# Differential attention: coefficients once per head, scores one step ahead, five items beside the value slice, and the last rotations inside the loop

## The chip, the core and the metric

The kernel runs on one core of a Trainium2 chip. The metric is the device time of one execution in microseconds (us). In the profile PE is TensorE (matmul), PEld its weight loads, DVE is VectorE, ACT is ScalarE, POOL is GpSimd and SP is SyncE.

## What is computed

The program is one inference step of a four-layer transformer trunk on 384 tokens (128 context tokens and 256 latent tokens), model width 1024. Each layer is a token mixer followed by a SwiGLU network, both modulated by shift, scale and gate vectors from a linear map of a condition (`w_ada`). Only layer 0, differential attention, is touched by the change:

```
q, k, v = split(h @ w_qkv)                    # 1024 columns each
q = rms_norm(q per 64), k = rms_norm(k per 64)
q, k = apply_rope(q), apply_rope(k)           # latent tokens only
s = einsum(q[head, map], k[head, map]) / 8    # 8 heads, 2 maps each
p = softmax(s)
a = p[map 0] - lam * p[map 1]
o = rms_norm(a @ v[head]) * 0.2 * gain
out = o @ w_o
```

Context queries see the 128 context keys, latent queries see 128 cached and 256 latent keys.

## The kernel before, in words

**Projection.** Weights arrive in units of 1024 columns, are cast by ScalarE (`wh`, L234), and VectorE subtracts the cast for the low part (`wl`, L244). Three matmuls per product (high x high, low x high, high x low) restore precision. In layer 0 `proj_slices` computes four slices of 512 columns, in eight steps k each: queries 0 to 511, keys 512 to 1023, queries 512 to 1023, and last the second half of the values, here called the **value slice**. What a slice leaves to do (`post`, `post_norm`: statistics, a scaling L878, the rotations L891 to L910, the transposes L918 and their copies L923) is a list of functions, and the next slice calls one of them in each of its steps. The value slice accumulates in PSUM banks 3, 5 and 7, and after it ScalarE copies these out (`put_v`, L944).

**Attention.** There are 24 **items**: 8 heads, and for each three blocks of 128 queries in the order 1, 2, 0. Blocks 1 and 2 have 384 keys (wide items), block 0 has 128 (narrow items). For an item two score matmuls (L977, one per map) fill two of four banks; VectorE takes two maxima (L991); ScalarE does two exponentials with their sums (L1000); VectorE forms the reciprocal of one sum (L1005), the coefficient (L1009) and the combination of the two maps (L1015); TensorE transposes it (L1032), ScalarE copies that (L1034), TensorE multiplies by the values (L1063). After a head's last item come sums of squares on ScalarE (L1091), a chain of small operations on three numbers (L1105 to L1115), a scaling (L1117), a transpose (L1127) and the split into `oh` (L1128) and `ol` (L1129), the input of the output projection `w_o` (L396 to L398).

**Order.** `at(e, rank, f)` puts a function into **step** e, and `advance()` issues one step, sorted by rank. PE, DVE and ACT run exactly in the order written, in the loop. `IL0` says how many steps are issued in each k of the value slice; the rest run in a loop of their own up to step 24, and what is left is called between the first matmuls of `w_o`.

**Fill.** Products of the `w_ada` map are mixed in by `fill`. Some entries run on TensorE: a product (L337), a copy on ScalarE (L340), a turn (L346), a copy on VectorE (L347). Others are two passes of VectorE over 128x1024 numbers (L328). The small transposes, products and turns share a ring `tr` of two banks, 6 and 7.

Of the kernel before, what the change touches and what calls it, by code (L numbers as in the profile page):

```python
# [42 lines left out]
IL0 = (0,0,0,0,0,0,1,0)  # L43
ADA_PE = ((4, 0), (4, 1), (4, 3), (4, 4), (4, 5), (4, 7), (3, 0), (3, 1), (3, 3), (3, 4), (3, 5), (3, 7))
ADA_QKV = ((0, 0, 1, 0, 0, 0, 1, 0),) * 4
ADA_A = (((0.5,1),),((0.5,1),),((1.6,2),),(),((0.5,1),),((1.6,2),))
# [13 lines left out]
RK = (1.0, 1.1, 1.2, 1.3, 1.5, 2.5, 5.5)  # L60
DBANKS = dict(acc=(4, 5, 1, 2, 3), tr=(7, 0, 6))
RMS_AT = 1
ATT_A = (2, 3, 1, 1, 2, 1, 0)
# [86 lines left out]
def trunk(ctx: ExitStack, tc: tile.TileContext, a):  # L150
# [161 lines left out]
    def ada_parts():  # L312
# [31 lines left out]
        def turn(row):  # L344
            t = tbank()
            T.matmul(out=t[:, 0:2], lhsT=row, rhs=quarter, start=True, stop=True)  # L346
            V.tensor_copy(out=out, in_=t[:, 0:2])  # L347
# [6 lines left out]
        if pe:  # L354
            row = []
            return [lambda: row.append(product()), lambda: (turn(row[0]), finish())]
# [406 lines left out]
    def attn_layer(li, att, nd):  # L763
# [184 lines left out]
        def post(i, ps):  # L948
            if diff:
                if i == 3:  # L950
                    return [put_v(ps, 0, 512, 512), lambda: None]
                return post_norm(ps, i % 2, 512, 8, i // 2 * 4 + i % 2 * 4)
# [4 lines left out]
        events, state, out, last = {}, {}, {}, [None]  # L957

# [5 lines left out]
        def stats_of(c):  # L964
            if ("st", c) not in state:
                state["st", c] = sm.tile([128, 8, 6], F32, name="ast", tag="ast", bufs=3)
# [26 lines left out]
        def exps(i, c, t):  # L993
            st_ = stats_of(c)
            state["p", i] = []
            for m, ps in enumerate(state.pop(("s", i))):
                j = 2 * t + m
                w = ps.shape[1]
                p = att.tile([128, TOK + 1], F32, name="p", tag="p")
# [3 lines left out]
        def inverse(i, c, t):  # L1003
            j = slice(2 * t + int(diff), 2 * t + 2)
            V.reciprocal(out=stats_of(c)[:, 2, j], in_=stats_of(c)[:, 1, j])  # L1005

        def coefficient(i, c, t):
            st_ = stats_of(c)
            V.scalar_tensor_tensor(out=st_[:, 2, 2 * t:2 * t + 1], in0=st_[:, 1, 2 * t:2 * t + 1], scalar=neglam,  # L1009
                                   in1=st_[:, 2, 2 * t + 1:2 * t + 2], op0=ALU.mult, op1=ALU.mult)  # L1010
# [124 lines left out]
        def fill(what):  # L1135
# [3 lines left out]
            elif what and ad["done"] < min(len(adas), ad["limit"]):  # L1139
                pe = adas[ad["done"]][3]  # L1140
                f, f2 = ada_parts()
                f()
                (half_done if pe else halves).append(f2)

        def fill_end():
            while half_done:
                half_done.pop()()
# [559 lines left out]
```

## Time and profile before

| | |
|---|---|
| median of three runs | 1896.53 us (1895.76 to 1897.22) |
| profiled execution, its own time | 1896.06 us |
| its span, first to last instruction | 1894.3 us |
| PE busy in the span | 1867.7 us (99%) |
| DVE / ACT busy in the span | 1518.5 us / 901.6 us |
| first score matmul / last one | 125.4 us / 185.6 us |

The span leaves out 1.8 us around the first and the last instruction. Times inside a profile count from the start of the span.

### The profile page before, as it was taken

How to read it: one execution, taken by the hardware profiler on the slowest of the kernel's cores; microseconds unless marked ns; L12 is line 12 of the kernel's file. 1: busy time of each engine (PE TensorE's matmuls, PEld its weight loads, DVE VectorE, ACT ScalarE, POOL GpSimd, SP SyncE). 2: the span in 40 equal slices, each digit the busy share in tenths (PEclk: the TensorE clock that was granted, in tenths of full speed). 3: DMA queues.
4: the chain of work that ended last, by engine and by line, in shares of the span. 5: the costliest groups of instructions: out<-in, count | busy, mean ns of one | idle time of the engine just before them, and what ended most of it. 6: DMA issues, size and time to landing. Idle time of an engine off the chain costs nothing.

```text
span 1894.3 us, 29902 instructions
## 1 busy us (share of the span) xinstructions
PE 1867.7 (99%) x11200; PEld 1744.2 (92%) x11200; DVE 1518.5 (80%) x2980; ACT 901.6 (48%) x1764; POOL 109.3 (6%) x207
## 2 busy tenths in 40 slices
PE   9998999999999999999999999999999999999999
PEld 6876999999975999999975999999989989999999
DVE  6999899995688999994688999994758897964442
ACT  6458553233558553234468553233556665632331
POOL 0011001110000001110000001110000000000000
PEclk9999999999999999999999999999999999999999
DMA  9664568775330568774330558774433324554442
GB/s 374 221 190 141 156 191 261 259 258 165 112 117 1 173 187 263 256 256 144 109 117 1 178 187 269 248 240 128 122 112 119 108 87 140 170 167 129 120 126 67
DMA packets 90742, 315.93 MB, mean 167 GB/s; under 512 B 10977, under 2 KB 14945, under 8 KB 90341
## 3 DMA queue, kind: packets, MB, share of 16 engines
q1 hardware_dynamic: 63508, 217.86, 35.7%
q0 software_dynamic: 26656, 95.97, 16.3%
q8 instruction: 88, 1.44, 0.3%
q14 instruction: 58, 0.47, 0.1%
q10 hardware_dynamic: 432, 0.20, 0.0%
HBM read 309.78 MB, written 4.20 MB: 166 GB/s over the span
## 4 chain that ended last, share of the span: by engine, by line
PE 87%; DVE 6%; ACT 4%; issue 2%; DMA 1%; POOL 0%; ACTq 0%; DVEq 0%; SPq 0%; POOLq 0%
PE b L396 24%; PE b L398 24%; PE b L397 24%; PE b L629 2%; PE b L630 2%; PE b L633 2%; PE b L515 2%; ACT p L1000 1%; PE b L977 1%; PE b L1079 1%; DMA ada<-in_ada_dram 1%; PE b L1051 1%; DVE ast L991 1%; PE b L918 1%; DVE junk L328 1%
## 5 line engine op out<-in xcount | busy, mean ns | idle before, releaser
L244 DVE TENSOR_TENSOR wl<-raw,wh 128x1024 fp32r<-128x1024 f32 x384 | 467.3, 1222 | 155.3 <-ACT wh L234 154.9
L234 ACT CAST wh<-raw 128x1024 fp32r<-128x1024 f32 x384 | 399.2, 1047 | 352.4 <-PE b L397 201.2
L398 PE MATMUL b<-fhh,wl 128*128 128x384 f32 x1280 | 433.9, 339 | 0.0
L397 PE MATMUL b<-fhl,wh 128*128 128x384 f32 x1280 | 432.4, 338 | 0.0
L396 PE MATMUL b<-fhh,wh 128*128 128x384 f32 x1280 | 432.4, 338 | 0.0
L328 DVE CUSTOM_DVE_ANT_0 junk<-ada,condb 128x1024 bf16<-128x1024 f32 x312 | 380.3, 1219 | 2.6 <-DMA ada<-in_ada_dram 0.2
L398 PEld LDWEIGHTS b<-fhh,wl 128*128 128x128 f32 x1280 | 241.8, 189 | 0.0
L397 PEld LDWEIGHTS b<-fhl,wh 128*128 128x128 f32 x1280 | 241.8, 189 | 0.0
L396 PEld LDWEIGHTS b<-fhh,wh 128*128 128x128 f32 x1280 | 241.5, 189 | 0.0
L396 PE MATMUL b<-fh,wh 128*128 128x384 f32 x704 | 239.0, 339 | 0.0
L398 PE MATMUL b<-fh,wl 128*128 128x384 f32 x704 | 237.4, 337 | 0.0
L397 PE MATMUL b<-fl,wh 128*128 128x384 f32 x704 | 237.4, 337 | 0.0
L700 ACT CAST fh<-w 128x384 fp32r<-128x384 f32 x88 | 45.2, 514 | 288.8 <-DVE w L706 280.8
L396 PE MATMUL b<-xh,wh 128*128 128x386 f32 (+1 forms) x448 | 155.1, 346 | 0.0
L398 PE MATMUL b<-xh,wl 128*128 128x386 f32 (+1 forms) x448 | 152.6, 341 | 0.0
L397 PE MATMUL b<-xl,wh 128*128 128x386 f32 (+1 forms) x448 | 151.5, 338 | 0.0
L299 POOL DMA_DIRECT2D ada<-in_ada_dram x176 | 93.4, 531 | 985.5 <-DVE mod L328 840.4
L398 PEld LDWEIGHTS b<-fh,wl 128*128 128x128 f32 x704 | 132.3, 188 | 0.0
L397 PEld LDWEIGHTS b<-fl,wh 128*128 128x128 f32 x704 | 132.2, 188 | 0.0
L396 PEld LDWEIGHTS b<-fh,wh 128*128 128x128 f32 x704 | 132.2, 188 | 0.0
L413 DVE SCALAR_TENSOR_TENSOR x<-b,mod,x 128x128 f32<-128x128 f32 x192 | 69.6, 411 | 40.3 <-PE b L398 40.3
L706 DVE TENSOR_TENSOR w<-b,w 128x384 f32<-128x384 f32 x80 | 44.4, 555 | 58.4 <-PE b L398 58.2
(267 smaller groups left out, 2850.5 us busy)
## 6 DMA issues: line engine op xcount, KB each, us to landing
raw<-in_w_dram SPq DMA_DIRECT2D x384, 512.0 KB, 4.2
ada<-in_ada_dram POOLq DMA_DIRECT2D x176, 512.0 KB, 4.7
a0s<-in_ada_dram SPq DMA_DIRECT2D x8, 512.0 KB, 9.8
ada<-in_ada_dram SPq DMA_DIRECT2D x8, 512.0 KB, 9.9
x<-in_x_dram SPq DMA_DIRECT2D x4, 384.0 KB, 4.7
out_y_dram<-x SPq DMA_DIRECT2D x8, 192.0 KB, 1.9
condb<-saved SPq DMA_DIRECT2D x1, 1024.0 KB, 11.4
s<-in_state_dram POOLq DMA_DIRECT2D x8, 128.0 KB, 2.3
```

Of the source, the lines that this page charges most:

```text
L234: S.copy(out=hi, in_=st["raw"][u])
L244: V.tensor_tensor(out=lo, in0=st["raw"].pop(u), in1=st["hi"][u].bitcast(F32), op=ALU.subtract)
L299: (nc.gpsimd if i >= 16 else nc.sync).dma_start(out=t, in_=a["ada"][i])
L328: V.tensor_tensor_reduce(out=ad["junk"], in0=raw, in1=ad["cond"][:, j, :], op0=ALU.mult, op1=ALU.add, scale=1.0, scalar=0.0, accum_out=out ...
L396: T.matmul(out=out, lhsT=lh, rhs=rh, start=start, stop=False)
L397: T.matmul(out=out, lhsT=lh, rhs=rl, start=False, stop=False)
L398: T.matmul(out=out, lhsT=ll, rhs=rh, start=False, stop=stop)
L413: V.scalar_tensor_tensor(out=x[:, d, c0:c1], in0=ps[:, c0:c1], scalar=gate[:, d, j:j + 1], in1=x[:, d, c0:c1], op0=ALU.mult, op1=ALU.add)
L515: T.matmul(out=ps[3 * i + t], lhsT=xs[:, k, t * 128:t * 128 + 128], rhs=ws, start=p == 0 and k == 0, stop=p == 2 and k == KC - 1)
L629: T.matmul(out=ps[t], lhsT=hh[:, k, c], rhs=wh, start=k == 0, stop=False)
L700: S.copy(out=fh[:, j, :], in_=m)
L706: V.tensor_tensor(out=m, in0=up[:, :TOK], in1=sg, op=ALU.mult)
```

## The change

- The reciprocals and coefficients of a head's three items are formed by one operation each (`coefficients`), two steps after the head's last item was issued.
- Scores are issued one step ahead: maxima and exponentials of item i move from step i to step i+1, the combination from i+1 to i+4, the transpose from i+2 to i+5, the product with the values from i+3 to i+6.
- Steps 0 to 4 are issued in k = 3 to 7 of the value slice (before: step 0 in k = 6).
- The rotations and transposes of the last query slice leave the value slice and are called one per step after steps 5 to 10.
- `fill` is called once per step from step 5 on, and the turn of a TensorE entry and its copy are placed one step later, at ranks 0.4 and 1.6.
- The second map's exponentials go to the ring `w`, and the statistics have five buffers in another pool.

```diff
-IL0 = (0,0,0,0,0,0,1,0)
+IL0 = (0,0,0,1,1,1,1,1)
-ADA_A = (((0.5,1),),((0.5,1),),((1.6,2),),(),((0.5,1),),((1.6,2),))
+ADA_FROM = 5
-RK = (1.0, 1.1, 1.2, 1.3, 1.5, 2.5, 5.5)
+RK = (1.0, 1.1, 1.2, 1.3, 1.5, 0.4, 1.6)
-ATT_A = (2, 3, 1, 1, 2, 1, 0)
+ATT_A = (5, 6, 4, 1, 1, 1, 0)
...
-            return [lambda: row.append(product()), lambda: (turn(row[0]), finish())]
+            return [lambda: row.append(product()), lambda: row.append(turn(row[0])), lambda: (keep(row[1]), finish())]
...
+                fs = post_norm(ps, i % 2, 512, 8, i // 2 * 4 + i % 2 * 4)
+                if i == 2:
+                    turns.extend(fs[3:4] + fs[6:7] + fs[4:5] + fs[7:8] + fs[2:3] + fs[5:6])
+                    return fs[:2]
+                return fs
...
-                p = att.tile([128, TOK + 1], F32, name="p", tag="p")
+                p = work(TOK) if diff and m else att.tile([128, TOK + 1], F32, name="p", tag="p", bufs=6 if diff else 7)
...
-        def coefficient(i, c, t):
+        def coefficients(c):
             st_ = stats_of(c)
-            V.scalar_tensor_tensor(out=st_[:, 2, 2 * t:2 * t + 1], in0=st_[:, 1, 2 * t:2 * t + 1], scalar=neglam,
-                                   in1=st_[:, 2, 2 * t + 1:2 * t + 2], op0=ALU.mult, op1=ALU.mult)
+            V.reciprocal(out=st_[:, 2, 1:6:2], in_=st_[:, 1, 1:6:2])
+            V.scalar_tensor_tensor(out=st_[:, 2, 0:6:2], in0=st_[:, 1, 0:6:2], scalar=neglam,
+                                   in1=st_[:, 2, 1:6:2], op0=ALU.mult, op1=ALU.mult)
...
-                at(i + 1, RK[0], inverse, *args)
-                at(i, RK[1], maxima, 0, *args)
-                at(i + 1, RK[2], coefficient, *args)
-                at(i, RK[3], maxima, 1, *args)
-                at(i + 1, RK[4], combine, *args)
-                at(i, 3, exps, *args)
-                for rank, what in ADA_A[i % len(ADA_A)]:
-                    at(i, rank, fill, what)
-                at(i + int(RK[6] < 0), abs(RK[6]), fill_end)
+                at(i + 1, RK[1], maxima, 0, *args)
+                if i % 3 == 2:
+                    at(i + 2, 1.0, coefficients, c)
+                at(i + 1, RK[3], maxima, 1, *args)
+                at(i + cl, RK[4], combine, *args)
+                at(i + 1, 3, exps, *args)
+                if i >= ADA_FROM:
+                    at(i, 2.6, fill, 2)
+                at(i + 1, RK[5], fill_end, 0)
+                at(i + 1, RK[6], fill_end, 1)
...
-            pend = proj_slices(li, hh, hl, list(enumerate(slice_cols(li))), post, ids, step, pend)
+            pend = proj_slices(li, hh, hl, list(enumerate(slice_cols(li))), post, ids, step, pend) + turns
```

Lines below L347 have other numbers in the changed file: L977 is L986 there, L991 L1000, L1000 L1009, L1015 L1026, L1032 L1043, L1063 L1074, L944 L947, L629 to L633 are L632 to L636, L347 L350 and L1129 L1140. The new reciprocal is L1019, the new coefficient L1020.

ScalarE where the value slice ends and the loop begins, before: the last transposed queries (`qT`), the three copies of the values, a row of a fill product, the two exponentials of item 1 and those of item 2.

```order
L923 COPY qT<-b_1312 128x4x128
L944 COPY vt<-b_1138 128x512
L944 COPY vt<-b_1139 128x512
L944 COPY vt<-b_1140 128x512
L340 COPY row<-b_1339 128x128
L1000 ACTIVATE p,ast<-b_1335,ast 128x384
L1000 ACTIVATE p,ast<-b_1336,ast 128x384
L1000 ACTIVATE p,ast<-b_1364,ast 128x128
L1000 ACTIVATE p,ast<-b_1365,ast 128x128
```

The same place after the change: the exponentials of item 3, the copies of the values, a row, those of item 4, the first transposed item, a second row and those of item 5.

```order
L1009 ACTIVATE p,ast<-b_1272,ast 128x384
L1009 ACTIVATE w,ast<-b_1273,ast 128x384
L947 COPY vt<-b_1138 128x512
L947 COPY vt<-b_1139 128x512
L947 COPY vt<-b_1140 128x512
L340 COPY row<-b_1335 128x128
L1009 ACTIVATE p,ast<-b_1297,ast 128x384
L1009 ACTIVATE w,ast<-b_1298,ast 128x384
L1045 COPY pt<-b_1352 128x384
L340 COPY row<-b_1373 128x128
L1009 ACTIVATE p,ast<-b_1328,ast 128x128
L1009 ACTIVATE w,ast<-b_1329,ast 128x128
```

The exponentials of items 0 to 3 now stand ahead of the copies of the values, and those of item 4 behind them and behind the row of a product.

VectorE in the middle of the loop before, two steps of one head: small operations stand between the two maxima of an item.

```order
L347 COPY mod<-b_1770 128x2
L1005 RECIPROCAL ast<-ast 128x1
L991 TENSOR_REDUCE ast<-b_1773 128x1
L1009 SCALAR_TENSOR_TENSOR ast<-ast,lam 128x1
L991 TENSOR_REDUCE ast<-b_1774 128x1
L1015 SCALAR_TENSOR_TENSOR p<-p,ast 128x384
L328 ISA junk,mod<-ada,condb 128x1024
L328 ISA mod 128x1
L1129 SCALAR_TENSOR_TENSOR ol<-b_1793,subg,oh 128x384
L1005 RECIPROCAL ast<-ast 128x1
L991 TENSOR_REDUCE ast<-b_1804 128x1
L1009 SCALAR_TENSOR_TENSOR ast<-ast,lam 128x1
```

VectorE at the corresponding two steps after the change.

```order
L350 COPY mod<-b_1742 128x2
L1000 TENSOR_REDUCE ast<-b_1738 128x1
L1000 TENSOR_REDUCE ast<-b_1739 128x1
L1026 SCALAR_TENSOR_TENSOR p<-w,ast,p 128x384
L350 COPY mod<-b_1783 128x2
L328 ISA junk,mod<-ada,condb 128x1024
L328 ISA mod 128x1
L1140 SCALAR_TENSOR_TENSOR ol<-b_1800,subg,oh 128x384
L1000 TENSOR_REDUCE ast<-b_1779 128x1
L1000 TENSOR_REDUCE ast<-b_1780 128x1
```

The reciprocal and the coefficient are gone from these steps; one pair of them stands at the head of every third step.

TensorE in the value slice after the change, from the start of k = 4 (bank numbers 1138 to 1140 are the value slice's accumulators, 1209 and 1210 the scores of item 0, 1222 and 1223 those of item 1).

```order
L986 MATMUL b_1223<-kT,qT 128x384
L632 MATMUL b_1138<-wh,hh 128x512
L633 MATMUL b_1138<-wl,hh 128x512
L632 MATMUL b_1139<-wh,hh 128x512
L633 MATMUL b_1139<-wl,hh 128x512
L986 MATMUL b_1209<-kT,qT 128x384
L986 MATMUL b_1210<-kT,qT 128x384
L632 MATMUL b_1140<-wh,hh 128x512
L986 MATMUL b_1222<-kT,qT 128x384
```

Before, no scores stood here; the first ones stood between k = 5 and k = 6.

## Rows read from the trace of the kernel before

**Rows 1.** Windows by stage: each engine's busy us, PE clock, DMA share.

```profile
104.00:125.00 21.00, 21.00 (x100) 17.16 (x99) 21.00 (x36) 7.57 (x13) 1.61 (x3) 1.00 0.68 214
125.00:132.30 7.30, 7.30 (x52) 4.93 (x50) 5.58 (x12) 4.52 (x10) 1.06 (x2) 1.00 0.49 150
132.30:186.00 53.70, 46.16 (x452) 32.03 (x452) 48.84 (x178) 42.80 (x176) 7.95 (x15) 1.00 0.48 150
186.00:200.00 14.00, 14.00 (x92) 13.85 (x92) 11.14 (x33) 6.73 (x27) 1.59 (x3) 1.00 0.54 175
```

**Rows 2.** DVE groups by line and shape, 132 to 186 us: busy, mean ns, idle before.

```profile
L991 DVE TENSOR_REDUCE ast<-b 128x1 f32<-128x384 f32 x30 | 16.4, 547 | 1.4 <-PE b L977 1.3
L1015 DVE SCALAR_TENSOR_TENSOR p<-p,ast 128x384 f32<-128x384 f32 x15 | 9.1, 609 | 0.0
L328 DVE CUSTOM_DVE_ANT_0 junk<-ada,condb 128x1024 bf16<-128x1024 f32 x7 | 8.5, 1219 | 0.2 <-DMA ada<-in_ada_dram 0.2
...
L991 DVE TENSOR_REDUCE ast<-b 128x1 f32<-128x128 f32 x14 | 3.9, 277 | 0.0
L1005 DVE RECIPROCAL ast<-ast 128x1 f32<-128x1 f32 x21 | 3.4, 160 | 3.1 <-ACT p L1000 2.9
L1117 DVE TENSOR_TENSOR osb<-b,ast 128x384 f32<-128x384 f32 x6 | 3.3, 550 | 0.0
...
L1015 DVE SCALAR_TENSOR_TENSOR p<-p,ast 128x128 f32<-128x128 f32 x7 | 2.4, 345 | 0.0
```

**Rows 3.** Timeline of DVE inside a step: start us, us, engine, line, operation.

```profile
166.95 0.15 DVE L1005 RECIPROCAL ast<-ast 128x1 f32<-128x1 f32 x1
167.02 0.54 DVE L991 TENSOR_REDUCE ast<-b 128x1 f32<-128x384 f32 x1
167.48 0.21 DVE L1009 SCALAR_TENSOR_TENSOR ast<-ast,lam 128x1 f32<-128x1 f32 x1
167.61 0.55 DVE L991 TENSOR_REDUCE ast<-b 128x1 f32<-128x384 f32 x1
```

**Rows 4.** Timeline of PE, value slice: first matmuls of k = 4 and 5.

```profile
120.63 0.39 PE L629 MATMUL b<-wh,hh 128*128 128x512 f32 x1
...
122.73 0.40 PE L629 MATMUL b<-wh,hh 128*128 128x512 f32 x1
```

**Rows 5.** Timeline of DVE beside it: the last query slice's scaling and first rotation.

```profile
121.02 1.87 DVE L878 TENSOR_TENSOR xh<-b,rq 128x512 f32<-128x512 f32 x3
...
123.41 0.68 DVE L906 TENSOR_TENSOR w<-xh,rope 128x512 f32<-128x512 f32 x1
124.01 0.68 DVE L908 TENSOR_TENSOR w<-xh,rope 128x512 f32<-128x512 f32 x1
```

**Rows 6.** Timeline of PE and ACT where the value slice ends.

```profile
131.90 1.56 ACT L944 COPY vt<-b 128x512 f32<-128x512 f32 x3 [0.28 <-PE b L633]
...
132.26 0.92 PE L977 MATMUL b<-kT,qT 64*128 64x384 f32 x4
...
133.10 0.64 PE L337 MATMUL b<-ada,condP 128*32 128x128 f32 x16
...
133.87 0.27 ACT L340 COPY row<-b 128x128 f32<-128x128 f32 x1 [0.41 <-PE b L337]
134.03 0.59 ACT L1000 ACTIVATE p<-b,ast 128x384 f32<-128x384 f32 x1
...
134.60 0.58 ACT L1000 ACTIVATE p<-b,ast 128x384 f32<-128x384 f32 x1
```

**Rows 7.** Timeline of PE where the output projection begins.

```profile
185.82 0.44 PE L396 MATMUL b<-oh,wh 128*128 128x384 f32 x1
...
186.45 0.49 PE L1032 MATMUL b<-ident,p 128*128 128x128 f32 x3
...
188.54 0.83 PE L1063 MATMUL b<-vt,pt 128*128 128x128 f32 x6
```

**Rows 8.** Timeline of DVE: the last operation of step 23.

```profile
188.51 0.61 DVE L1129 SCALAR_TENSOR_TENSOR ol<-b,subg,oh 128x384 fp32r<-128x384 f32 x1
```

More of the change, by code (lines that the diff above doesn't have):

```diff
@@ L346, in turn, with keep @@
             T.matmul(out=t[:, 0:2], lhsT=row, rhs=quarter, start=True, stop=True)
+            return t
+        def keep(t):
             V.tensor_copy(out=out, in_=t[:, 0:2])
@@ L950, in post @@
                 if i == 3:
-                    return [put_v(ps, 0, 512, 512), lambda: None]
-                return post_norm(ps, i % 2, 512, 8, i // 2 * 4 + i % 2 * 4)
+                    return [put_v(ps, 0, 512, 512)]
+                fs = post_norm(ps, i % 2, 512, 8, i // 2 * 4 + i % 2 * 4)
[3 more added lines that the diff above has]
+                return fs
             if i == 1:
@@ L957, in attn_layer @@
         events, state, out, last = {}, {}, {}, [None]
+        turns = []
         def at(e, rank, f, *args):
@@ L965, in stats_of @@
             if ("st", c) not in state:
-                state["st", c] = sm.tile([128, 8, 6], F32, name="ast", tag="ast", bufs=3)
+                state["st", c] = att.tile([128, 8, 6], F32, name="ast", tag="ast", bufs=5 if diff else 3)
             return state["st", c]
@@ L1003, in inverse @@
         def inverse(i, c, t):
-            j = slice(2 * t + int(diff), 2 * t + 2)
+            j = slice(2 * t, 2 * t + 2)
             V.reciprocal(out=stats_of(c)[:, 2, j], in_=stats_of(c)[:, 1, j])
-        def coefficient(i, c, t):
+        def coefficients(c):
             st_ = stats_of(c)
-            V.scalar_tensor_tensor(out=st_[:, 2, 2 * t:2 * t + 1], in0=st_[:, 1, 2 * t:2 * t + 1], scalar=neglam,
-                                   in1=st_[:, 2, 2 * t + 1:2 * t + 2], op0=ALU.mult, op1=ALU.mult)
+            V.reciprocal(out=st_[:, 2, 1:6:2], in_=st_[:, 1, 1:6:2])
+            V.scalar_tensor_tensor(out=st_[:, 2, 0:6:2], in0=st_[:, 1, 0:6:2], scalar=neglam,
+                                   in1=st_[:, 2, 1:6:2], op0=ALU.mult, op1=ALU.mult)
         def combine(i, c, t):
@@ L1140, in fill, with fill_end @@
                 pe = adas[ad["done"]][3]
-                f, f2 = ada_parts()
+                f, *fs = ada_parts()
                 f()
[L1143 to L1147, printed above, removed]
+                if pe:
+                    half_done.append(fs)
+                else:
+                    halves.append(fs[0])
+        def fill_end(step=None):
+            for fs in [fs for fs in half_done if step is None or len(fs) == 2 - step]:
+                while fs:
+                    fs.pop(0)()
+                    if step is not None:
+                        break
+                if not fs:
+                    half_done.remove(fs)
         n_items = len(items)
@@ L1580, in trunk @@
     class Att:
-        BUFS = dict(xh=3, p=7)
+        BUFS = dict(xh=3)
         def __init__(self, pool):
```

## The prediction

> **What bounds the kernel now.** I read the windows by stage first, to find where TensorE (PE) is not full. From 104 to 132 us, in the slices, and again from 186 us, in the output projection, PE is busy without a gap [rows 1]. Between them, in the attention loop from 132.3 to 186.0 us, it is busy for 46.16 of 53.70 us: 7.5 us of idle, the only place that the change can win from. No edit touches another layer, so 7.5 us, 0.4% of the kernel, is about the ceiling. Who holds PE up is in the same row: VectorE (DVE) is busy for 48.84 us and ScalarE (ACT) for 42.80. DVE is also full from 104 to 125 us, and has 1.7 us of idle in the next window. So DVE is what bounds the loop, and the groups by line say what it does: maxima, combinations, fill passes; and that it stands still 3.1 us before the reciprocals, nearly all of it for the exponentials, and 1.4 us before maxima for scores [rows 2].
>
> What an operation costs a full queue is the distance to the next start, not its duration. A wide maximum lasts 0.55 us and gives way after 0.46; a reciprocal gives way after 0.07 and a coefficient after 0.13 [rows 3]. So I take about 0.08 off the means of the larger operations: wide maximum 0.46, narrow 0.19, wide combination 0.53, narrow 0.27, scaling L1117 0.47, fill pass 1.15 [rows 2].
>
> **The change part by part.**
>
> *Small operations.* 24 reciprocals and 24 coefficients become 8 and 8. The new ones work on three numbers; nothing in the rows lets a second or third column cost anything. Saved: 16 x 0.07 + 16 x 0.13 = 3.2 us of DVE, on the engine that bounds. The upper bound is the full durations, 16 x 0.16 + 16 x 0.21 = 5.9 us; the lower bound is nothing, if they stood in waits. Only 3 us of DVE wait lie in the loop, so I keep 3.2. The Trainium skill (VectorE: DVE Perf Modes, section on the TRN2 errata) gives every VectorE instruction a fixed cost of about 150 cycles, which is an estimate of 0.156 us each and 5.0 us for the 32. The measured start distances are shorter and decide; by the page the time would be 1.8 us lower.
>
> *Steps 0 to 4 beside the value slice.* At the start of k = 4, 120.63 us [rows 4], the order puts a first score on bank 4, which is free, and those on banks 0, 1 and 2 behind four and more value matmuls. These banks come free as DVE scales the last queries from 121.02 to 122.89 us, 0.6 us for each [rows 5]. So I take no PE wait here (the bound is 1.1 us, until the first scaling ends). A k lasts 2.10 us [rows 4], a wide pair of scores 0.84 (132.26 to 133.10), a narrow one half [rows 6]. The slice then ends at 120.63 + 4 x 2.10 + 4 x 0.84 + 0.5 = 132.9 us, where before it ended at 132.26 with one item done. The four items' scores are PE work moved, not removed; three query transposes move the other way.
>
> *What ACT meets at the hand-over.* This is the new wait. The exponentials of item 4 could start when their maxima are done, about 131.7 us (its scores end one k before the slice, at 130.8, and two maxima take 0.92). In ACT's order they stand behind the three copies of the values, which wait for the end of the slice, and behind the row of the first product, L340. That product is the first user of the ring `tr` after it becomes (7, 6), so it takes bank 7, the one that the last copy of the values frees. Before, that copy ended 1.2 us after the slice (131.90 + 1.56 against 132.26), now then at 134.1. The product starts there, the row follows 0.77 us after the product's start (133.10 to 133.87) and the exponentials 0.16 after that [rows 6]: 135.05. Two of them take 2 x 0.64, to 136.35. The scores of item 6 want the banks that these free, so PE stands still for some 1.4 us around them, ending at 136.8; then a turn (0.25), the second product and its row: 138.0. Behind it stand the narrow exponentials of item 5 (0.72), and behind these, on DVE, the coefficients of head 1: about 138.8 us. DVE has done the rotation, the maxima of item 5 and a combination by about 134.8 and stands still for 4.0 us.
>
> The Trainium skill (PSUM — Partial Sum Buffer, section on engine and sequencer instructions) says that ScalarE's queue is a strict FIFO, and this rule speaks against the change: nothing overtakes the waiting copies. In the rows too ACT goes copies, row, exponentials. If item 4 could overtake, the entry would come 2.8 us earlier and the sum below would be lower by as much; I go by the rows.
>
> *The loop from there.* In steps 7 to 23 of the changed order I count on DVE: 24 wide and 10 narrow maxima (13.0 us), 12 wide and 5 narrow combinations (7.7), 8 fill passes (9.2), the second rotation and the context queries' gain, four operations of 0.60 as [rows 5] (2.4), 26 small ones of the head's norm at 0.08 (2.1), 5 scalings and 5 splits `ol` (5.0), 6 pairs of coefficients (1.2), 12 small copies and additions (0.9): 41.5 us. Because exponentials are now a step older when they are wanted, I leave 0.25 us of wait for each of 5.7 heads: 1.4. Step 23 then ends at 138.8 + 41.5 + 1.4 = 181.7 us on DVE; before it ended at 188.51 + 0.53 = 189.0 [rows 8].
>
> *What that is worth on PE.* PE reaches the output projection when it has transposed item 18, for which a bank must be freed by DVE's small copy in step 22; behind that copy stand 4.3 us of DVE work in steps 22 and 23. So 181.7 - 4.3 + 1.0 for transposes and one product with values = 178.4 us, against 185.82 before [rows 7]. These 7.4 us are not all gain: with the longer pipeline PE still owes two more transposes (0.49 and a third of it), two more products with values (0.83 each) and one fill product with its turn (0.9), 3.2 us by [rows 6, 7]. Left: 4.2 us. The rotations' transposes and the moved scores are in the slice's and loop's times already.
>
> *Coupling.* PE then has 46.2 - 3.0 (scores moved out) - 3.2 (owed) + 1.4 (transposes moved in) = 41.4 us of work for the 45.5 us between 132.9 and 178.4, ACT about 38. Three engines at 85 to 94% that wait for each other through two banks lose something that no row of before gives; bounds are nothing and the 7.5 us that PE lost before. Before, at DVE's 91%, waits cost DVE 4.9 us of 53.7, and I have charged 1.4 + 4.0. I take 1.2 more. Gain: 4.2 - 1.2 = 3.0 us.
>
> *The end.* Head 7 must reach the projection before its k = 7. DVE's leftovers after step 23 (three combinations, two head norms, four fill passes, four low splits) are some 15 us, so to about 197; PE needs the head at about 201. Hidden, with 4 us to spare. Buffers (six for `p`, five for the statistics, the ring `w` of five, which the rotation also uses) are asked for again only after their last reader in the order; cost nothing.
>
> Against the profiled execution's 1896.06 us the sum gives 1893.1; that execution lies 0.5 us under the median of 1896.53, so the forecast is 1893.4, between the two.
>
> **The rivals.** 0.2% of the kernel, 3.8 us, is about what a measurement can tell from no change; "faster" begins below 1892.7 and "slower" above 1900.3.
>
> *A. Faster.* The entry stall is shorter, or the small operations cost their full durations. For it: the 2.7 us between 3.2 and 5.9, and the 1.2 us of coupling that I only assumed. Against it: the start distances. Gain 5.5 to 6.5, time about 1890.5. Chance 0.22.
>
> *B. No gain, the stall takes it.* If the entry costs DVE 7 us and not 4 (another round through the row copy), the 3 us are gone: 1896.3. For it: each round of product, row and exponentials is about 3.5 us. Against it: by step 7 PE stands a step ahead. Chance 0.18.
>
> *C. Slower.* The two-bank ring. The copy of a turned product (L347) now stands behind the combination on DVE, and PE's next transpose needs that bank, so PE is tied to DVE in each of 11 product pairs, and the next step's scores stand behind it in PE's queue. After the copy PE needs about 2.0 to 2.8 us (transpose, product with values, scores, turn, product) and DVE's next step gives it 2.0 to 3. If each pair costs 0.7 us, 7.7 us are lost against 4.2 won: 1900. It decides from 0.4 us a pair on, and makes the kernel slower by 0.2% from 0.75. Against it: scores are a step ahead, which covers one late step. Chance 0.10, of which 0.08 above 1900.3.
>
> **How the numbers follow.** The likeliest, a DVE-bound loop that starts late and then runs shorter, has 0.50; its own range is 1891.5 to 1895.5, and a good third of it lies below 1892.7. Faster: 0.50 x 0.35 + 0.21 = 0.39; slower 0.08; same 0.53. For 8 in 10 the range takes A in to 1890.0 and B and the mild part of C up to 1897.0.
>
> **What would show it.** In the changed profile: no PE wait for the first scores, and the slice's end at 132.9 us; one DVE wait of about 4 us near 135 to 139, for exponentials, at L1019; later heads at 7.1 us or less with short waits at L1019; the projection's first matmul (L399) near 178; PE full after it. Wrong would be: no such wait (A), waits of PE at L1043 for L350 or for the copies `pt` all through the loop (C), or PE gaps after 180 us, which would mean that the late heads are not hidden.

## The result and the profile after

The changed kernel takes 1909.38 us (median of 4 runs, 1908.24 to 1910.90) against 1896.28: 13.1 us or 0.69% slower (ratio 1.0069, 95% interval 1.0057 to 1.0081). The forecast was 1893.4, with 1890.0 to 1897.0. The profiled execution took 1909.67 us, 13.6 more than that of before.

All of the loss arises in the one attention block that was changed. The first product of the feed-forward part behind it, on VectorE (DVE), comes here in the kernel before and here in the changed one (start, duration):

```profile
257.79 0.55 DVE L706 TENSOR_TENSOR w<-b,w 128x384 f32<-128x384 f32 x1
```

```profile
272.31 0.56 DVE L709 TENSOR_TENSOR w<-b,w 128x384 f32<-128x384 f32 x1
```

That is 14.5 us later; 0.9 us come back over the rest of the kernel. The windows of the changed kernel (stretch and its length in us; busy us of PE, PEld, DVE, ACT, POOL, with the number of instructions; granted clock; DMA) answer to [rows 1]; the second is the loop from the first of its coefficients to the end of step 23:

```profile
132.30:186.00 53.70, 46.18 (x380) 30.53 (x376) 39.34 (x115) 32.23 (x127) 7.11 (x14) 0.94 0.42 129
142.50:197.40 54.90, 46.97 (x394) 32.64 (x394) 43.70 (x131) 36.32 (x149) 6.62 (x13) 0.97 0.41 126
```

In the window from 132.3 us DVE was busy for 48.84 us before and ScalarE (ACT) for 42.80; now it is 39.34 and 32.23. TensorE (PE) is as busy as before and gets less done: 380 matmul records against 452, though some of its work has moved ahead of the window. So no engine is full: the loop is no longer bound by the work of one, but by what each waits for from the others. The ends of heads show the pace: the first one before, then the first and the fifth of the changed kernel (answers to [rows 8]). The row below them is the first matmul of the output projection (answers to [rows 7]):

```profile
151.27 0.61 DVE L1129 SCALAR_TENSOR_TENSOR ol<-b,subg,oh 128x384 fp32r<-128x384 f32 x1
```

```profile
161.78 0.62 DVE L1140 SCALAR_TENSOR_TENSOR ol<-b,subg,oh 128x384 fp32r<-128x384 f32 x1 [2.80 <-ACT oh L1139]
...
196.87 0.62 DVE L1140 SCALAR_TENSOR_TENSOR ol<-b,subg,oh 128x384 fp32r<-128x384 f32 x1
```

```profile
195.47 0.45 PE L399 MATMUL b<-oh,wh 128*128 128x384 f32 x1 [1.22 <-ACT p L1009]
```

Four heads lie between these two: 35.1 us, 8.8 us a head. Before, five heads took 37.2 us (151.27 to 188.51), 7.45 a head. So these four heads lost 5.3 us, and the first of them was already 10.5 us late (161.78 for 151.27), with the entry and the longer pipeline in it. The operation at 196.87 us is the last of step 23, which ends at about 197.4 us; the forecast was 181.7. Seen from PE, the output projection begins 9.7 us later than before (195.47 for 185.82 [rows 7]), and from there to the product of the feed-forward part it takes 76.8 us where it took 72.0. Of these 4.9 us the prediction had charged 3.2, as work that PE still owes.

*The entry.* PE's timeline, and then ACT's and DVE's, where the value slice ends (answers to [rows 4] and [rows 6]):

```profile
120.84 0.91 PE L986 MATMUL b<-kT,qT 64*128 64x384 f32 x2
...
122.81 0.92 PE L986 MATMUL b<-kT,qT 64*128 64x384 f32 x4
...
124.09 0.91 PE L986 MATMUL b<-kT,qT 64*128 64x384 f32 x2
...
135.01 0.49 PE L986 MATMUL b<-kT,qT 64*128 64x128 f32 x4
136.27 0.64 PE L337 MATMUL b<-ada,condP 128*32 128x128 f32 x16 [0.77 <-ACT vt L947]
...
137.88 1.97 PE L986 MATMUL b<-kT,qT 64*128 64x384 f32 x4 [0.48 <-ACT p L1009]
```

```profile
134.66 1.56 ACT L947 COPY vt<-b 128x512 f32<-128x512 f32 x3 [3.11 <-PE b L636]
136.98 0.27 ACT L340 COPY row<-b 128x128 f32<-128x128 f32 x1 [0.76 <-PE b L337]
137.15 0.59 ACT L1009 ACTIVATE p<-b,ast 128x384 f32<-128x384 f32 x1
...
141.50 0.27 ACT L340 COPY row<-b 128x128 f32<-128x128 f32 x1 [2.74 <-PE b L337]
```

```profile
140.40 0.16 DVE L350 COPY mod<-b 128x2 f32<-128x2 f32 x1 [3.44 <-PE b L346]
142.50 0.18 DVE L1019 RECIPROCAL ast<-ast 128x3 f32<-128x3 f32 x1 [1.94 <-ACT w L1009]
```

PE stands nowhere for the first scores, as forecast. The slice ends at 135.0 us for 132.9. One reason is in the first three rows: the two maps of an item are matmuls of 64 rows, and when both are ready they start together, so that four take 0.92 us; one map by itself (two matmuls) takes 0.91. The first two items come as 2, 4 and 2 matmuls, three times 0.84 us from start to next start where the prediction counted two. Also a k behind scores takes 2.28 us (from 132.73 to 135.01) for 2.10. Then follow, as the prediction has it, copies, product, row and exponentials, then a second product with its row and exponentials, and at the end L1019: DVE stands still for 5.4 us (3.44 + 1.94; forecast 4.0) and starts at 142.5 for 138.8. In this stretch the windows show what PE did and the clock that it was granted:

```profile
134.00:138.00 4.00, 2.75 (x29) 1.67 (x28) 2.93 (x7) 2.58 (x7) 1.08 (x2) 1.00 0.37 146
138.00:140.00 2.00, 2.00 (x5) 0.69 (x6) 0.00 (x0) 0.76 (x3) 0.00 (x0) 0.68 0.72 195
140.00:144.00 4.00, 4.00 (x31) 3.51 (x31) 1.62 (x6) 1.35 (x6) 0.53 (x1) 0.50 0.36 82
144.00:146.00 2.00, 2.00 (x9) 0.78 (x8) 0.40 (x1) 1.62 (x5) 0.00 (x0) 0.61 0.41 166
146.00:148.00 2.00, 2.00 (x17) 1.64 (x17) 1.85 (x5) 0.37 (x3) 0.00 (x0) 1.00 0.00 0
```

PE stands for 1.25 us of the four from 134; then the granted clock falls from 2.4 to 1.2 GHz (0.50), and from 146 us it is up again: 2 x 0.32 + 4 x 0.50 + 2 x 0.39 = 3.4 us of clock are lost, where the kernel before lost none in its loop. The pair of scores at 137.88 takes 1.97 us where it took 0.92 [rows 6]; in it are the lower clock and a second map that starts 0.56 us behind the first.

*A head in the steady part.* The chain of waits through one head (start, us, what):

```profile
168.16 0.48 DVE ast L1000
...
168.66 0.67 ACT p L1009 x2
169.34 0.56 ACT w L1009 x2
169.90 0.37 ACT pt L1045
170.27 0.49 ACT oh L1139
...
170.78 0.63 DVE ol L1140
...
171.46 0.69 PE b L337 x16
...
172.22 0.27 ACT row L340
172.49 0.36 ACT p L1009 x2
172.85 0.36 ACT w L1009 x2
...
173.23 0.19 DVE ast L1019
```

DVE's maximum releases the exponentials; behind these, in ACT's order, stand the copies `pt` and `oh`; DVE's next operation L1140 wants `oh`; it gives a bank of `tr` back, which PE's product wants; ACT copies its row, and the next exponentials stand behind that copy; for these DVE waits again, at L1019. The chain runs from one engine to the next all the way, in 5.1 us. DVE's waits behind the first L1019, from 142.8 to 197.4 us (us in total, times, longest):

```profile
DVE ol L1140 <- ACT oh L1139: 5.9, 3, 2.8
DVE mod L350 <- PE b L346: 2.9, 3, 1.7
DVE ast L1019 <- ACT w L1009: 1.1, 3, 0.5
```

### The profile page after: what moved, and what is told of

It is laid out like the page before. It is cut to its first block, busy times and chain, and to the rows that moved or that the text cites. A ratio compares the mean times of both kernels' runs of the same rounds, so it can differ in the third digit from the quotient of the medians.

```text
span 1907.9 us, 29847 instructions
## 1 busy us (share of the span) xinstructions
PE 1878.8 (98%) x11200; PEld 1748.6 (92%) x11200; DVE 1516.7 (79%) x2948; ACT 901.3 (47%) x1764; POOL 109.3 (6%) x207
## 4 chain that ended last, share of the span: by engine, by line
PE 89%; DVE 5%; ACT 5%; issue 1%; DMA 0%; DVEq 0%; ACTq 0%
PE b L399 24%; PE b L401 24%; PE b L400 24%; PE b L632 3%; PE b L633 3%; PE b L636 3%; PE b L518 2%; PE b L986 2%; ACT p L1009 1%; PE b L1090 1%; PE b L1062 1%; PE b L921 1%; DVE ast L1000 1%; PE b L1074 0%; PE b L1523 0%
## 5 line engine op out<-in xcount | busy, mean ns | idle before, releaser
L244 DVE TENSOR_TENSOR wl<-raw,wh 128x1024 fp32r<-128x1024 f32 x384 | 467.5, 1222 | 152.9 <-ACT wh L234 152.3
```

The costliest lines, as they stand in the source:

```text
L244: V.tensor_tensor(out=lo, in0=st["raw"].pop(u), in1=st["hi"][u].bitcast(F32), op=ALU.subtract)
```

## The experiments

The theories were: 1, a chain through the four score banks and the row copy; 2, the two banks of `tr`, with L350 behind the combination; 3, the entry and the half clock; 4, a cost of the other two parts by themselves; 5, DVE's wait at L1140. All times are medians of four or more runs; the ratio is to the kernel before, whose median was 1895.9 to 1896.2 throughout. The ratios' intervals are 0.1 to 0.2% wide to either side, so of two changed kernels a difference under some 3 us may be chance.

**One part alone, on the kernel before.** Scores a step ahead:

```diff
-                at(i, RK[1], maxima, 0, *args)
+                at(i + 1, RK[1], maxima, 0, *args)
...
-                at(i, 3, exps, *args)
+                at(i + 1, 3, exps, *args)
...
-ATT_A = (2, 3, 1, 1, 2, 1, 0)
+ATT_A = (3, 4, 1, 1, 2, 1, 0)
```

> The kernel before with scores a step ahead alone (maxima and exponentials one step behind their scores, and all that follows them one step later); coefficients by item, one item beside the slice and rotations ahead of the loop as before. Theory 1 (serial chain through score banks and row copy): slower by 5 to 9 us, 1901 to 1906, and TensorE waits at the row's product chain as in the changed kernel. Theory 2 (two transposition banks with L350 late) and theory 3 (entry): the hand-over of the ring is that of before, within 2 us of 1896.3. Theory 4 (coefficients once per head or rotations in the loop cost by themselves): no change here, 1895 to 1898.

1905.55 us, ratio 1.0049 (1.0034 to 1.0063): 9.7 us lost by this part alone, with heads of 8.4 us (158.15 to 200.12 us, five heads). A pair of scores in PE's timeline of this run, and ACT's beside it:

```profile
162.28 1.38 PE L977 MATMUL b<-kT,qT 64*128 64x384 f32 x4
```

```profile
161.28 0.58 ACT L1000 ACTIVATE p<-b,ast 128x384 f32<-128x384 f32 x1
162.02 0.58 ACT L1000 ACTIVATE p<-b,ast 128x384 f32<-128x384 f32 x1
```

A pair of wide scores takes 0.92 us when both banks are free, and 1.38 when the second map must wait for its bank: the one at 162.28 starts behind the exponential of 161.28, and its second map only at 162.74, when that of 162.02 has ended. In the kernel before every wide pair from 125 us on takes 0.92. In all, the scores' weight loads waited for exponentials 16 times from 118 to 200 us (before: once, 0.2 us):

```profile
PEld b L977 <- ACT p L1000: 5.7, 16, 1.1
```

Most of this is no idle time of PE: while the second map waits, the first one runs, and behind it the second one alone. The scores' busy time and the mean of one matmul (ns) from 120 us to the feed-forward part, before, in the changed kernel and here:

```profile
L977 PE MATMUL b<-kT,qT 64*128 64x384 f32 (+1 forms) x96 | 18.6, 464 | 0.0
```

```profile
L986 PE MATMUL b<-kT,qT 64*128 64x384 f32 (+1 forms) x96 | 24.1, 483 | 1.5 <-ACT p L1009 1.5
```

```profile
L977 PE MATMUL b<-kT,qT 64*128 64x384 f32 (+1 forms) x96 | 27.5, 487 | 2.6 <-ACT p L1000 2.4
```

One matmul lasts hardly longer; the two maps run less often side by side. Not all of the 9.7 us is the banks, however: this trace, too, has a stretch at half clock behind gaps (PE is busy for 2.42 of the four us from 134), which the kernel before has not in its loop:

```profile
138.00:142.00 4.00, 3.67 (x22) 1.77 (x24) 3.23 (x12) 1.18 (x5) 0.00 (x0) 0.67 0.10 40
142.00:146.00 4.00, 4.00 (x30) 3.38 (x19) 1.18 (x5) 2.23 (x7) 0.53 (x1) 0.50 0.42 130
```

Coefficients once per head alone (combination, transposition and product with the values two steps later, buffers as in the change), and the same with the output's turn ahead of the exponentials:

```diff
-                at(i + 1, RK[0], inverse, *args)
+                if i % 3 == 2:
+                    at(i + 1, RK[0], coefficients, c)
...
-                at(i + 1, RK[4], combine, *args)
+                at(i + 3, RK[4], combine, *args)
...
-ATT_A = (2, 3, 1, 1, 2, 1, 0)
+ATT_A = (4, 5, 1, 1, 2, 1, 0)
```

```diff
-                    at(f + FIN[-1][0] + 1, r0 + 4.5, turn_o, c)
+                    at(f + FIN[-1][0] + 1, r0 + 2.5, turn_o, c)
```

> The kernel before with the reciprocal and coefficient once per head alone (combination two steps later, transposition and product with the values two steps later; scores, entry and rotations as before). Theories 1 to 3 put no cost here: 32 small VectorE instructions less (3.2 us) against two more steps at the loop's end, 1893 to 1898. Theory 4 (this part costs by itself, since the last head's combinations stand two steps later and w_o's last products with them): 1899 to 1905.

> The kernel before with coefficients once per head (1899.7 by itself) and the output's turn at rank 2.5. In the trace of that run the chain of waits goes scores - product - row copy - exponentials - pt copy - L1129's twin - L1130 once per head. Theory 5: the wait of VectorE (7.4 us in the loop) goes, 1893 to 1896, at or under the kernel before. Theory 1: what is left of the chain still ends at the next step's exponentials, 1898 to 1900.

1899.70 us (1.0018; 1.0009 to 1.0027) and 1899.03 (1.0015; 1.0006 to 1.0025). The part that was to save 3.2 us costs 3.6. DVE's wait for `oh` is not why: it is 7.1 us from 118 to 200 us in the first of these runs and gone from the list in the second, whose trace shows no half clock in the loop. In the first the heads go at 8.7 us (154.67 to 198.29, five), though the kernel loses only 3.6 us: the pace of heads in the loop is not the loss itself, since work behind the loop makes up for a part.

Five items beside the value slice alone:

```diff
-IL0 = (0,0,0,0,0,0,1,0)
+IL0 = (0,0,0,1,1,1,1,1)
```

> The kernel before with five items beside the value slice alone. Theory 3 (the entry costs by itself: value copies ahead of exponentials, then half clock): 3 to 6 us slower, 1899 to 1902. Otherwise the VectorE work of four items is hidden beside the slice, which itself gets longer by their matmuls: 1892 to 1896.

1910.37 us (1.0076; 1.0061 to 1.0091), worse than either theory had it. In this kernel the rotations and their transposes stand ahead of the value copies, and ACT does these copies 14 us later than before [rows 6]:

```profile
146.32 1.57 ACT L944 COPY vt<-b 128x512 f32<-128x512 f32 x3
```

The first products with values wait for them. So this number is not the price of the entry in the changed kernel, which does the rotations later; that one is below.

How much DVE's small operations are worth: the kernel before without its 24 reciprocals and 24 coefficients, with no step moved. The combination takes the plain factor lambda; the normalisation of the second map is left out.

```diff
-            V.scalar_tensor_tensor(out=p[0], in0=p[1], scalar=stats_of(c)[:, 2, 2 * t:2 * t + 1], in1=p[0],
+            V.scalar_tensor_tensor(out=p[0], in0=p[1], scalar=neglam, in1=p[0],
...
-                at(i + 1, RK[0], inverse, *args)
...
-                at(i + 1, RK[2], coefficient, *args)
```

> The kernel before without the reciprocal and the coefficient of each item: 48 small VectorE instructions less, 4.8 us of VectorE's time by the trace; the combination takes the plain factor lambda, so that the second map's normalisation is left out. No step moves. If the loop is bound by VectorE's work, as the prediction has it, 3.5 to 4.8 us less: 1891 to 1893. If it is bound by round trips between the engines, less than 2 us: 1894 to 1897.

1893.76 us (0.9987; 0.9977 to 0.9996): 2.3 us less between the medians, 0.8 to 4.4 by the interval, where the start distances of [rows 3] give 4.8 for the 48 operations; heads of 7.1 us (149.82 to 185.30, five). Its DVE groups and window:

```profile
L991 DVE TENSOR_REDUCE ast<-b 128x1 f32<-128x384 f32 x30 | 15.8, 550 | 3.2 <-PE b L977 2.8
```

```profile
132.30:186.00 53.70, 48.77 (x475) 34.91 (x475) 48.58 (x145) 44.36 (x188) 8.45 (x16) 1.00 0.49 155
```

DVE is as full as before (48.58 us) and waits 2.8 us for scores where it waited 1.3 [rows 2]. The time lies between the two forecasts: DVE's work bound the kernel before in part, and when it shrinks a part comes back as wait for PE.

**One part undone, on the changed kernel.** The entry of before, the rotations ahead of the loop, and scores in the step of their maxima (with all behind them one step earlier):

```diff
-IL0 = (0,0,0,1,1,1,1,1)
+IL0 = (0,0,0,0,0,0,1,0)
```

```diff
-                    turns.extend(fs[3:4] + fs[6:7] + fs[4:5] + fs[7:8] + fs[2:3] + fs[5:6])
-                    return fs[:2]
+                    return fs
```

```diff
-                at(i + 1, RK[1], maxima, 0, *args)
+                at(i, RK[1], maxima, 0, *args)
...
-                at(i + 1, 3, exps, *args)
+                at(i, 3, exps, *args)
...
-ATT_A = (5, 6, 4, 1, 1, 1, 0)
+ATT_A = (4, 5, 3, 1, 1, 1, 0)
```

> The changed kernel with one item beside the value slice as before (in place of five). Theory 3 (entry stall and the half clock behind it are most of the 13 us): 6 to 12 us less, 1898 to 1903. Theory 1 (the chain in each step): the heads stay at 8.8 us; the entry's stall goes, and four items come back into the loop at some 2.2 us each: 1907 to 1913.

> The changed kernel with the last queries' rotations and transpositions ahead of the loop again, beside the value slice as before. Theory 4 (rotations in the loop cost by themselves): 2 to 4 us less, 1905 to 1907. Theories 1 to 3: the loop keeps its 8.8 us a head less some 0.3 us for the VectorE work taken out, and the value slice gets VectorE and ScalarE work that delays the first items: 1907 to 1911.

> The changed kernel with maxima and exponentials back in the step of their scores and everything behind them one step earlier (coefficients once per head, first five items beside the slice and rotations in the loop stay). Theory 1 (serial chain through the score banks and the row copy): the bank dependency spans two steps again, 7.5 us a head, 6 to 10 us less than the changed kernel, 1900 to 1903. Theory 2 (two transposition banks with L350 late): the ring is as it was, 1907 to 1910. Theory 3 (entry stall and half clock): five exponential pairs now stand ahead of the value copies, so that the entry stall shrinks by up to 3 us and the clock may stay up: 1903 to 1906 with heads still at 8.8 us.

The entry: 1905.40 us (1.0048; 1.0031 to 1.0065), 4.0 us back, with no half clock in the loop and the same pace of heads. The rotations: 1906.19 (1.0053; 1.0038 to 1.0068), 3.2 back. The scores: 1919.02 (1.0122; 1.0107 to 1.0137), 9.6 us more, against theory 1. Its waits from 118 to 200 us say why:

```profile
DVE ast L1000 <- PE b L986: 16.6, 14, 3.0
...
PEld b L1043 <- DVE mod L350: 9.1, 8, 1.9
```

Here the ring `tr` closes a chain: DVE waits for scores, the copy L350 stands behind its maxima and combination, L1043 waits for the bank, and the next scores stand behind L1043. With L350 between the maxima it opens:

```diff
-RK = (1.0, 1.1, 1.2, 1.3, 1.5, 0.4, 1.6)
+RK = (1.0, 1.1, 1.2, 1.3, 1.5, 0.4, 1.15)
```

> The earlier run with scores in the step of their maxima (1919 us) with L350 between the two maxima in place of behind the combination. If that run was slow because of a serial chain scores - maxima - combination - L350 - L1043 - next scores (theory 2, the two-bank ring), it falls by 8 to 14 us, to 1905 to 1911. If the ring is not the cause, 1917 to 1920.

1909.96 us (1.0076; 1.0061 to 1.0091), 9.1 us less, which is the changed kernel's own time. And in the changed kernel itself the same edit is no gain:

> The changed kernel with the copy L350 of the modulation product (which frees its transposition bank) between the two maxima of its step on VectorE, in place of behind the combination; nothing else moves. Theory 2 (two-bank ring: L1043 waits for L350) expects most of the 6.4 us that the trace shows of such waits at L1043 to go: 3 to 6 us less, 1903 to 1906. Theory 1 (the chain through score banks and row copy alone) expects no more than 1 us: 1908 to 1910.

1912.06 us (1.0087; 1.0072 to 1.0102). The waits of L1043 for L350 are gone from the list, but now the second maximum stands behind L350, which waits for its turn L346 (9.0 us in 7 waits from 118 to 200 us, for 6.4 in 4 without the edit); the exponentials come later, and the scores' busy time goes from 24.1 to 27.2 us. The 6.4 us of the expectation add the waits of L1043's weight loads, 3.9 us, and of its matmuls, 2.5 us, in the same number of places; the edit could not win both.

These two runs differ in one thing, the scores' step, and by 2.1 us (1909.96 in their step, 1912.06 a step ahead), which may be chance. So with the other parts in place no run shows a gain from taking the scores back.

**One wait taken away, in the changed kernel.** The product behind the exponentials of its step, then the scores last in their step, then the latter with the entry of before:

```diff
-                    at(i, 2.6, fill, 2)
+                    at(i, 3.5, fill, 2)
```

```diff
-            at(i, 0, scores, *args)
+            at(i, 5.5 if diff else 0, scores, *args)
```

> The changed kernel with the modulation product issued behind the exponentials of its step (rank 3.5 for 2.6): on ScalarE the row copy L340 now stands behind the two exponentials, all else as it was. Theory 1 (serial chain: with scores a step ahead the four score banks make the scores of step e wait for the exponentials issued in step e-1, those stand behind the row copy L340, which waits for the product L337, which stands behind the scores of its own step on TensorE): the chain opens, heads fall from 8.8 us towards 7.5, and with six heads in the steady part the time falls by 6 to 10 us, to 1900 to 1903. Theory 2 (the two transposition banks: L350 behind the combination holds a bank that L1043 waits for): nothing in that changes, 1908 to 1910. Theory 3 (the entry stall and the half clock of TensorE behind it are most of the loss): only the one row copy at the entry goes, 1907 to 1909.

> The changed kernel with the two score matmuls issued at the end of their step (rank 5.5, behind the transposition L1043 and the product L1074) in place of at its start; nothing else moves. Theory 1 (the scores wait for the exponentials of two items before, and everything else of the step on TensorE stands behind them): the 5.5 us by which L986 is longer than before go, since the waiting scores hold nothing up that is ready; 1903 to 1906, with the entry as it is. Theory 2 (the transposition banks) and theory 3 (entry): 1908 to 1911. If the exponentials themselves are late because VectorE then waits for the scores, no gain either: 1907 to 1912.

> The same with one item beside the value slice as before. That entry alone gave 1905.4 without a stretch at half clock. Theory 1: 1899 to 1902. If the place of the scores is not what counts: 1904 to 1907.

The product: 1903.50 us (1.0040; 1.0025 to 1.0055), 5.9 us back, the largest gain of any single edit to the changed kernel; its last heads, at full clock, take 8.2 us. The scores wait there for exponentials almost as before the edit (3.6 us for 4.1 from 118 to 200 us); what goes is ACT's wait for the product, at the row copy (3.1 us in 3 waits for 10.9 in 9). The scores last: 1917.27 (1.0114; 1.0099 to 1.0129) and 1910.23 (1.0079; 1.0062 to 1.0096), 8 and 5 us worse than without the edit: the wait goes over to DVE, as the first of the two shows from 116 to 210 us:

```profile
DVE ast L1000 <- PE b L986: 15.6, 12, 3.3
```

The output's turn ahead of the exponentials, by the edit shown above, alone; the product behind the exponentials together with the entry of before; that pair with the output's turn; and that pair with L350 between the maxima:

> The changed kernel with a head's output transposition, its copy L1139 and its residual L1140 at rank 2.5 of their step, ahead of the product, the exponentials and the pt copy, in place of behind them (4.5). Theory 5 (VectorE stands at L1140 for L1139, which ScalarE does only behind two exponentials and the pt copy, and those exponentials waited for VectorE's own maxima: some 2 us a head): the 5.9 us of that wait in the loop go, 1903 to 1906. Theory 1 (the chain exponentials - scores - product - row copy) alone: VectorE then waits elsewhere for the same exponentials, 1907 to 1911.

> The changed kernel with the product behind the exponentials (1903.5 by itself) and one item beside the value slice (1905.4 by itself), L350 as it is. If both losses are separate, 1898 to 1901; if the gain of the first was partly that the stretch at half clock moved, 1902 to 1905.

> The same with the output's turn at rank 2.5 as well. Theories 1, 3 and 5 together, all repaired: heads near 7.5 us and 1894 to 1898. If heads stay over 8 us, something that none of the three names costs more than 3 us: 1900 to 1904.

> The changed kernel with three of its points altered at once: product behind the exponentials (6 us less by itself), one item beside the value slice as before (4 us less by itself, and no stretch at half clock), L350 between the maxima. If the first two add up, 1899 to 1900, and with 3 us for the copy 1896 to 1898; if the steps are then bound by VectorE as in the kernel before, heads of 7.5 us and 1894 to 1896; if scores a step ahead have a cost that none of the three touches, heads stay at 8.2 us and the time at 1900 to 1902.

1911.05 us (1.0078; 1.0061 to 1.0095), 1904.16 (1.0042; 1.0027 to 1.0057), 1908.74 (1.0061; 1.0046 to 1.0076) and 1909.84 (1.0079; 1.0062 to 1.0096). Theory 5 falls: the wait at L1140 goes, and DVE waits elsewhere, here in the third of these from 140 to 200 us:

```profile
DVE mod L350 <- PE b L346: 11.8, 9, 2.8
DVE ol L1140 <- ACT oh L1139: 1.7, 2, 0.8
```

The two repairs that gave 5.9 and 4.0 us by themselves give 5.2 together. That pair's trace has two stretches at half clock (0.50 from 134 to 138 and from 166 to 170 us), where the entry of before by itself has none in the loop.

**The half clock.** Four matmuls of no use in the gap at the end of the value slice:

```diff
+            if diff:
+                dm = bank_at(6)
+                for _ in range(4):
+                    T.matmul(out=dm[:, :TOK], lhsT=qT[0:64, 0, 0:128], rhs=kT[0:64, 0, 0:TOK], start=True, stop=True)
             ring["tr"][0] = (7, 6)
```

> The changed kernel with four matmuls of 64x384 ahead of the scores of the sixth item, at the end of the value slice, into the free transposition bank; their result isn't used. They fill some 1.7 us in which TensorE stands and put the sixth item's scores back by at most that. If the half clock that follows (139 to 146 us in the trace) comes from this gap and is a cost of its own, the stretch goes or shortens and the time falls by 1.5 to 3 us, to 1906 to 1908. If the clock falls all the same, 1909 to 1911. If it stays up and the time doesn't fall, the loop is bound by other waits there.

1910.58 us (1.0073; 1.0058 to 1.0088), no gain. The windows:

```profile
134.00:138.00 4.00, 4.00 (x32) 2.46 (x31) 2.15 (x6) 1.50 (x4) 0.55 (x1) 1.00 0.19 71
138.00:146.00 8.00, 7.43 (x60) 5.02 (x59) 3.89 (x12) 4.94 (x18) 1.06 (x2) 1.00 0.44 131
146.00:148.00 2.00, 0.58 (x4) 0.42 (x4) 1.97 (x5) 0.13 (x1) 0.00 (x0) 1.00 0.00 0
148.00:154.00 6.00, 5.49 (x32) 3.62 (x31) 4.36 (x15) 4.37 (x20) 1.06 (x2) 0.51 0.38 100
```

With the gap filled the clock stays up through 146 us. Then PE stands for 1.42 of 2 us, and the stretch at half clock comes there. So this run doesn't show what the clock by itself costs.

## Why the prediction was wrong

Right were: the cheap start of the first scores; the new wait at the hand-over, its order (copies, row, exponentials, L1019) and that the queue lets nothing overtake. The Trainium skill (PSUM — Partial Sum Buffer, section on engine and sequencer instructions) says so, and the trace agrees: the fifth item's exponentials start at 137.15 us, 0.17 after L340 has started, though their maxima ended at 133.85. The wait was sized at 4.0 us and measured 5.4; with the slice 2.1 us longer and the second round at half clock DVE came 3.7 us late.

The step that failed is "the loop from there", with "coupling". It counted 41.5 us of DVE work from L1019 to the end of step 23; the window shows 43.7, so the work was counted well. To this it added 1.4 us of wait, and 1.2 for coupling. Measured are 54.9 - 43.7 = 11.2 us of wait. Step 23 ended 15.7 us late: 3.7 from the entry, 2.2 from work, 9.8 from waits. The prediction took for granted that DVE, having bound the loop before, would go on to bind it. The premise held in part for the kernel before (48 small operations less are worth 2.3 of 4.8 us) and not for the changed one. On PE the same step shows as a projection that begins 17.1 us later than forecast (195.47 for 178.4); the work owed behind it was put at 3.2 us and measured 4.9. The clock, 3.4 us of it lost at the entry, has no term in the sum.

What makes the waits is shown only in part. The scores a step ahead are one cause: a bank of scores is held from the score to its exponential. With four banks and two a step, exponentials in the step of their scores leave the banks free a whole step before they are wanted; one step later they are wanted at once. Scores then wait for the exponentials issued just before, 16 times in the run with this part alone, which costs 9.7 us, its stretch at half clock included. The place of the fill's product is another: the exponentials stand behind the row copy, the row behind the product, and the product moved behind the exponentials gives 5.9 us back. But neither is the whole of it: with L350 between the maxima in both, the changed kernel is no faster with the scores in their step (1909.96 against 1912.06). The prediction named this dependence only at the entry ("the scores of item 6 want the banks that these free") and let it go in the loop ("scores are a step ahead, which covers one late step").

Rival C (slower, 1900, chance 0.10) had the side right. Its sign was there: the weight loads of L1043 waited for L350 five times, 3.9 us. But freeing L350 early made the changed kernel no faster (1912.06), and the same edit put the second maxima behind the turn's wait, so this run doesn't decide how much the ring costs there; that the ring `tr` is a bound is shown only where the scores are not ahead (1919.02 to 1909.96).

The small operations, 3.2 us, are over-priced: 2.3 of 4.8 us of such a saving arrive, and with the combination two steps later the part costs 3.6 us. A sign of it stood in [rows 2]: 3.1 us of DVE's idle time lay right before the reciprocals, so that a part of what was taken away stood in a wait. The prediction took these some 3 us for all of DVE's wait in the loop, where the window that it uses later has 4.9 (53.70 - 48.84). The Trainium skill (VectorE: DVE Perf Modes, TRN2 errata) would have it at 5.0 us for 32, an estimate from its fixed cost; the run without 48 of them gave 2.3 us, and the measurement decides.

What is not settled: the parts don't add (alone they cost 9.7, 3.6 and 14.2 us, and together 13.1), and three single waits that were taken away (L350, L1140, scores ahead of the step's other matmuls) each came back in another place. Which edit would bring the loop back to 7.45 us a head with scores ahead was not found; none of the runs that keeps all of the computation beats the kernel before. More banks for the scores were not tried: all eight are in use. Nor was the new schedule of the fill run by itself (one entry in every step, its turn and copy a step later), or the coefficients by item put back into the changed kernel.

## What to carry to other kernels

Before an operation is moved a step ahead of its reader, count for how many steps its buffer is then held against how many there are: with four banks and two a step, "one step ahead" means "wanted at once". A sum of one engine's work forecasts a loop only while that engine stays full; when work is taken off it, follow one round through all queues (here maximum, exponentials, copy, residual, product, row, exponentials) and compare its length with what is left of the work. And a wait taken out of such a round should be expected to come back elsewhere until a trace shows the round itself shorter.

## What was not expected of the hardware

The granted clock of TensorE can be part of a loop's price. Where PE stands for 1.25 and for 1.42 us in the rows above, a stretch at 1.2 GHz follows; in the kernel before, with 1.34 us of idle between 133 and 140 us spread over several gaps, none did. Executions of one and the same kernel differ in this: the repair of product, entry and output took 1903.52 us at a mean clock of 0.996 and 1908.47 to 1909.59 at 0.993 and 0.992, and the product behind the exponentials 1902.09 at 0.998 and 1905.83 at 0.995. A thousandth of 1905 us is 1.9 us of lost clock, and with it the times differ by 1.2 to 1.8 us. By that the changed kernel's 0.995 against 0.997 would be 2 to 4 us of its 13. This is an estimate: the means are known to a thousandth, and a stretch at half clock comes with the gap ahead of it, so that no run parts the one's cost from the other's.

And a PE that waits for a bank can be busy all the same. The four matmuls of a wide pair take 0.92 us when the two maps start together, and one map by itself takes 0.91. So when the second bank is late the pair takes 1.38 us or more with no gap in it: the scores' busy time rose from 18.6 to 24.1 us, while one matmul lasted 483 ns for 464. PE's whole busy time from 120 us to the feed-forward part rose from 130.25 to 142.30 us for the same matmuls (942 and 944 records), the lower clock included, and the idle time only from 7.5 to 10.0.
